# Half-line pads in the SBUF tiles of a one-core diffusion-block kernel

## The chip, the cores and the metric

The kernel runs on one NeuronCore of a Trainium2 chip. The metric is the time of one execution on the device in microseconds (us). Before the change three runs gave 1022.84, 1023.95 and 1025.29 us, median 1023.95 us.

## The reference, cut to what matters

One block of a diffusion backbone runs over 256 latent tokens and 256 context tokens of width 1024; only the latent stream is returned.

```python
x   = x   + 0.5 * g1x * swiglu(modulate(rmsnorm(x, n1), sh1x, sc1x), w13_1, w2_1)     # 512 tokens:
ctx = ctx + 0.5 * g1c * swiglu(modulate(rmsnorm(ctx, n1), sh1c, sc1c), w13_1, w2_1)   # x and ctx
q, k, v, g, f, ga, gf = project(modulate(rmsnorm(x, n2), ...), w_in)                   # ctx: k, v only count
o = bidir_retention(rope(q), rope(k), v, ...)          # 4 heads, decays, states of the context
r = (silu(g) * groupnorm(o)) @ p_ret
fo = fft2(f).real @ p_four
x = x + g2x * ((sigmoid(ga) * r + sigmoid(gf) * fo) @ w_out)
x = x + 0.5 * g3x * swiglu(modulate(rmsnorm(x, n3), ...), w13_2, w2_2)
return rmsnorm(x, n_final)
```

All of it is in float32. The feed-forward width is 2816, `w_in` has 9216 columns.

## The kernel before

Activations stand transposed: 128 channels on the partitions, tokens along the free dimension, eight such tiles for 1024 channels. Every large product is done by `mm3` (lines 86 to 90): weight and activation are each split into a high part of the type float32r and the rest (`load_w`, lines 70 to 80, and `split`, lines 82 to 84), and three matmuls are added up in PSUM: low weight by high activation (L88), high by low (L89), high by high (L90). In each the 128 by 128 piece of weights is the stationary operand, loaded by an LDWEIGHTS of its own, and the activation streams past it. The activation has 512 columns where both streams run (the first feed-forward), 256 where one does, and 258 in the second feed-forward, whose tiles `hx` carry two more columns for a shift (line 856). In `fourier_in` the roles are exchanged: tokens are stationary and 512 columns of weights stream. In scores, `u_unit` and the Fourier units both operands are activations.

The stages, by the name of the bank that they write: `acc`, `pa`, `pb` (up, first feed-forward) and `y` (down), 512 columns; the last two column tiles of the second half of `y` are done as four units of 256 columns (`late`, lines 405 to 416). Then, with 256 columns: for each of four heads `kc`, `kx`, `q` (projections), `s` (scores), `u` (keys by scores, line 561), `o` (line 655), with the 512-column `f` in the last head; `g` (gates) among `sq` and `mx` (Fourier by tokens and by channels); `gg` and `ro` (merge); `yo` (output projection, line 865). Then `fa` and `fb` with 258 columns (22 units, line 890), and `z` with 256 (8 units of 66 matmuls, line 923). The order of instructions on each engine is made when the program is built, by a scheduler with a model of the chip; some matmuls of the next unit are drawn into the one before.

Weights come in pieces of 512 KB through one queue (SyncE) into `wr`, ScalarE makes the high part `wh`, VectorE (for some GpSimd) the low part `wl`; each has four buffers of 4096 bytes a partition.

**Where the tiles stand.** SBUF is given out in pools, from the left end (`per`, `wp`, `tp`, `hp`, `gp`, then `ttp` and `g2` in the place of `hp` and `gp`) and from the right (`mp`, `dp`, `mc`, `ap`, later `fp` and `mxp`), a pool's tiles one behind the other, each rounded up to 32 bytes. The place of a tile within a line of 128 bytes follows by addition. In this program all buffers of `wp` (`wr`, `wh`, `wl`) start 32 bytes into such a line; so do `h1`, `gh` and `gl`, `mg` (in the places of `tt`) and the first `hx`; all of their sizes but that of `hx` are whole lines, and so the places stay. `hx` tiles of 258 columns take 1032 bytes, rounded up to 1056, so that the sixteen stand at 32, 64, 96, 0, 32, ... ; behind them `g2h` and `g2l` are again at 32. `h2x` and `h2c`, all tiles of `ap` (`kt`, `qt`, `ut`, `pt`, `ht`), of `fp` (`dft`, `fu`, `cu`) and of `mxp` (`mx`, `gt`) stand at 96. Pieces of 128 columns of weights (512 bytes) and of 256 columns of activations (1024 bytes) are whole lines too, so a slice has its tile's place.

Of the kernel before, what the change touches and what calls it, by code (L numbers as in the profile page):

```python
# [8 lines left out]
F32R = mybir.dt.float32r  # L9
BF16 = mybir.dt.bfloat16  # L10
AF = mybir.ActivationFunctionType
ALU = mybir.AluOpType

P = 128
T = 256
D = 1024
KT = D // P
# [9 lines left out]
OUT = (P, KT, T)  # L27
UB = 4
HOOK = 0
TC_KW = dict(schedule_with_timeline_sim=True)  # L30


# [5 lines left out]
def block_kernel(ctx: ExitStack, tc: tile.TileContext, i: dict, out: bass.AP):  # L38
    nc = tc.nc
    V, S, G, PE = nc.vector, nc.scalar, nc.gpsimd, nc.tensor  # L40
# [9 lines left out]
    def fpool(stack, name, side):  # L50
        return stack.enter_context(tc.tile_pool(name=name, bufs=1, reuse_waits="tile", side=side))
# [4 lines left out]
    ada_stack = ExitStack()  # L56
    adp = fpool(ada_stack, "adp", "left")

    def bank(name):
        return psum.tile([P, 512], F32, name=name, tag="ps")  # L60

    def f32(ap):
        return ap.bitcast(F32)

    uid = [0]

    def wtile(t, name):
        return wp.tile([P, 1024], F32 if t == "wr" else F32R, name=name, tag=t, bufs=4)

    def load_w(src, n, lo_engine=None):  # L70

        uid[0] += 1
        raw, hi, lo = [wtile(t, f"{t}{uid[0]}") for t in ("wr", "wh", "wl")]
        dst = raw[:, :n]
        if len(src.shape) == 3:
            dst = dst.rearrange("p (k c) -> p k c", k=src.shape[1])
        nc.sync.dma_start(dst, src)
        S.copy(hi[:, :n], raw[:, :n])  # L78
        (lo_engine or V).tensor_tensor(lo[:, :n], raw[:, :n], f32(hi[:, :n]), op=ALU.subtract)  # L79
        return hi, lo  # L80

    def split(dst_hi, dst_lo, src):
        S.copy(dst_hi, src)
        V.tensor_tensor(dst_lo, src, f32(dst_hi), op=ALU.subtract)

    def mm3(o, w, a, start, stop):

        PE.matmul(o, w[1], a[0], start=start, stop=False)  # L88
        PE.matmul(o, w[0], a[1], start=False, stop=False)  # L89
        PE.matmul(o, w[0], a[0], start=False, stop=stop)  # L90

    def sl(pair, *idx):
        return pair[0][idx], pair[1][idx]
# [31 lines left out]
    for q in range(4):  # L125
        t = per.tile([P, 2, 512], F32, name=f"xs{q}")
# [33 lines left out]
    ct = stp.tile([P, 2, 4, 32], F32, name="ct")  # L160
    V.memset(ct, 0.0)
    ps = bank("ct")
    for c in range(4):
        PE.transpose(ps[:, c * P : (c + 1) * P], cr[:, c * P : (c + 1) * P], unit_raw)
# [156 lines left out]
    for k in range(KT):  # L321
# [3 lines left out]
        n = 2 * M1 * P  # L325
        hi, lo = wtile("wh", f"wh0_{k}"), wtile("wl", f"wl0_{k}")
# [16 lines left out]
    def some_ada(n):  # L343
        for _ in range(min(n, len(todo))):
            ada(*todo.pop(0))
# [12 lines left out]
                mm3(ps, sl(ws[k // 4], slice(None), slice(c, c + P)), h[k], k == 0, k == KT - 1)  # L358
        return gated_unit(pa, pb, f"1_{m}")

    def w2_chunks(src, kts):
        ws, k0 = [], 0
        for n in kts:
            w = load_w(src[:, k0 * P : (k0 + n) * P], n * P)
            ws += [sl(w, slice(None), slice(c * P, (c + 1) * P)) for c in range(n)]
            k0 += n
        return ws
# [3 lines left out]
    def add_sq(ap, cols, first, name):  # L371

        sq = tp.tile([P, 512], F32, name=f"sq{name}", tag="t2k", bufs=T2K)
        w = cols.stop - cols.start
        if first:
            S.activation(ssum[0][:, cols], ap, AF.Square)
            return
        S.activation(sq[:, :w], ap, AF.Square)  # L378
        G.tensor_tensor(ssum[0][:, cols], ssum[0][:, cols], sq[:, :w], op=ALU.add)  # L379

    def y_evac(ps, j, streams, st, col0):
        for n, s in enumerate(streams):
            c = slice(s * T, (s + 1) * T)
            V.scalar_tensor_tensor(
                xs[j][:, c], ps[:, col0 + n * T : col0 + (n + 1) * T], gate_col(st, s, j),
                xs[j][:, c], op0=ALU.mult, op1=ALU.add,
            )

    def ffn1_down(hf, gs, n_ada=0):
        late = []  # L390
        if hf:
            ssum[0] = per.tile([P, 512], F32, name="ssum2", tag="ssum")
        for j in range(KT):
            some_ada(n_ada)
            ws = w2_chunks(i["w2a"][hf, j], (6, 5))
            if hf and j >= KT - 2:
                late.append((j, ws))
                continue
            ps = bank(f"y{hf}_{j}")
            for k in range(HALF):  # L400
                mm3(ps, ws[k], gs[k], k == 0, k == HALF - 1)
            y_evac(ps, j, (0, 1), 0, 0)
            if hf:
                add_sq(xs[j], slice(0, 512), j == 0, f"2_{j}")
        for s in (0, 1):
            for j, ws in late:
                ps = bank(f"y{hf}_{j}_{s}")
                c = slice(s * T, (s + 1) * T)
                for k in range(HALF):
                    mm3(ps[:, :T], ws[k], sl(gs[k], slice(None), c), k == 0, k == HALF - 1)  # L410
                    if (s, j, k) == (1, KT - 2, 3):
                        norms.append(stage2_norm(0))
                y_evac(ps, j, (s,), 0, 0)
                sq = tp.tile([P, T], F32, name=f"sq2_{j}_{s}", tag="t1k", bufs=2)
                S.activation(sq, xs[j][:, c], AF.Square)
                late_sq[s].append(sq)
# [3 lines left out]
    def stage2_norm(s):  # L420
        ps = bank(f"st2_{s}")
        PE.matmul(ps[:, :T], ones, ssum[0][:, s * T : (s + 1) * T], start=True, stop=False)
        for n, sq in enumerate(late_sq[s]):
            PE.matmul(ps[:, :T], ones, sq, start=False, stop=(n == 1))
        return rstd_of(ps[:, :T], T, f"2_{s}")
# [54 lines left out]
    def decays(hd):  # L480
# [16 lines left out]
    raw = tp.tile([P, P], F32, name="unit_2", tag="t1k", bufs=2)  # L497
# [10 lines left out]
    ]  # L508

    ttp = fpool(ctx, "ttp", "left")  # L510
    tt = [ttp.tile([P, 512], F32, name=f"tt{n}", tag=f"tt{n}") for n in range(2 * HEADS)]
    ap = fpool(heads, "ap", "right")
    rope = ap.tile([P, 2, T], F32, name="rope")
    nc.sync.dma_start(rope, i["rope"])
    cos2, sin2 = [rope[:, n, :].unsqueeze(1).to_broadcast([P, 2, T]) for n in range(2)]
    keys, query, sums, probs = [
        [[ap.tile([P, 512], F32R, name=f"{nm}{n}_{x}") for x in range(2)] for n in range(cnt)]
        for nm, cnt in (("kt", 2), ("qt", 1), ("ut", UB), ("pt", 2))
    ]

    ht = [[ap.tile([P, D], F32R, name=f"ht{t}_{x}") for x in range(2)] for t in range(4)]

    def two(a):
        return a.rearrange("p (a t) -> p a t", a=2)
# [9 lines left out]
    def transposed(s, k, banks):  # L534

        for t in range(2):
            for x in range(2):
                if k % 4 == 0:
                    banks[t, x] = bank(f"ht{s}_{t}_{x}_{k}")
                c = slice((k % 4) * P, (k % 4 + 1) * P)  # L540
                PE.transpose(
                    banks[t, x][:, c].bitcast(F32R), (hc2, hx2)[s][k][x][:, t * P : (t + 1) * P], unit
                )
        if k % 4 == 3:
            c = slice((k // 4) * 512, (k // 4 + 1) * 512)
            for t in range(2):
                S.copy(ht[2 * s + t][0][:, c], banks[t, 0])
                S.copy(ht[2 * s + t][1][:, c], banks[t, 1])

    def first_unit(s, w, a, pss, hook=None):  # L550

        banks = {}
        for k in range(KT):
# [3 lines left out]
            transposed(s, k, banks)  # L557
            if hook and k == HOOK:
                hook()
# [122 lines left out]
    fs, fu, cu, mx = {}, [], [], []  # L682

    def fourier_open():
        heads.close()
        fs["fp"] = fp = fpool(mix, "fp", "right")
        dft = [fp.tile([P, 768], F32R, name=f"dft{n}") for n in range(2)]
        for n in range(2):
            raw = tp.tile([P, 512], F32, name=f"dftr{n}", tag="t2k", bufs=T2K)
            c = slice(n * 384, (n + 1) * 384)  # L690
            nc.sync.dma_start(raw[:, :384], i["dft"][:, c])
            split(dft[0][:, c], dft[1][:, c], raw[:, :384])
        fs["dft"] = dft
        for n in range(2):
            fu.append([[fp.tile([P, 512], F32R, name=f"fu{n}_{e}_{x}") for x in range(2)] for e in range(2)])
        fs["cu"] = [
            [fp.tile([P, 512], F32R, name=f"cu{n}_{x}") for x in range(2)] for n in range(4)
        ]
        mxp = fpool(mix, "mxp", "right")
        for tiles, nm, cnt in ((mx, "mx", 4), (gt, "gt", KT)):  # L700
            for n in range(cnt):
                tiles.append([mxp.tile([P, 512], F32R, name=f"{nm}{n}_{x}") for x in range(2)])
# [118 lines left out]
    for j in range(KT):  # L821
        ws = [load_w(i["wgate"][j, c], 1024) for c in range(2)]
# [6 lines left out]
        wr = [load_w(i["pret"][j, c], 1024) for c in range(2)]  # L829
# [26 lines left out]
    W = T + 2  # L856
    g2 = fpool(ctx, "g2", "left")
    hx = [
        (g2.tile([P, W], F32R, name=f"hxh{k}"), g2.tile([P, W], F32R, name=f"hxl{k}"))
        for k in range(KT)  # L860
    ]
    ssum[0] = per.tile([P, 512], F32, name="ssum3", tag="ssum")
# [60 lines left out]
    for j in range(KT):  # L923
        ws = w2_chunks(i["w2b"][j], (8, 8, 6))
# [124 lines left out]
```

## Time and profile before

| | |
|---|---|
| median of 3 runs | 1023.95 us |
| profiled execution | 1024.28 us, of which its span 1022.5 us |
| TensorE matmuls (PE) | 983.2 us busy, 96% of the span, 6792 instructions |
| weight loads (PEld) | 907.0 us, 89% |
| VectorE (DVE), ScalarE (ACT), GpSimd (POOL) | 65%, 46%, 6% |
| granted TensorE clock | 0.993 on average |
| HBM read | 164.70 MB, 162 GB/s over the span |

A row of a profile names the line of the kernel, the engine, the operation, output and inputs by tile names without numbers, the partitions and elements, the count, busy time and the mean duration of one in ns. The duration of a matmul contains its way through the array and overlaps that of its neighbours; how fast they follow each other is read from how many fall into a stretch.

### The profile page before, as it was taken

The numbers are of one execution on the slowest core, as the hardware profiler recorded it, in microseconds if no ns is written. First come the engines' busy times: TensorE is split into PE (matmuls) and PEld (weight loads), VectorE is DVE, ScalarE is ACT, GpSimd is POOL, SyncE is SP. The second block draws the span as 40 slices with busy tenths as digits, with TensorE's granted clock in tenths as the row PEclk, the third lists the DMA queues.
The fourth block names the chain that finished last, engine by engine and source line by source line (L and its number), as shares of the span: only waits on it lengthen the run. The fifth ranks groups of instructions, "written<-read, shape, count | busy, mean of one in ns | idle before, by whom it ended". The sixth has DMA issues, their size and how long they took to land.

```text
span 1022.5 us, 16777 instructions
## 1 busy us (share of the span) xinstructions
PE 983.2 (96%) x6792; PEld 907.0 (89%) x6792; DVE 661.5 (65%) x1083; ACT 469.1 (46%) x725; POOL 62.3 (6%) x39
## 2 busy tenths in 40 slices
PE   4899999999999999999999998999999989999996
PEld 3668888888888889899999997999999989999995
DVE  7938999998332434875575637955555767667543
ACT  5444232223422423755476457754445545554541
POOL 0000000000000013100000007000000210000011
PEclk9999999999999999899999999999999999999999
DMA  8727766996232233224132625455666555656651
GB/s 345 246 76 250 226 208 197 317 409 235 83 111 70 86 89 110 83 85 125 60 124 63 201 65 163 125 172 187 197 186 187 165 164 171 186 181 174 185 179 42
DMA packets 49238, 166.84 MB, mean 163 GB/s; under 512 B 5380, under 2 KB 7044, under 8 KB 49160
## 3 DMA queue, kind: packets, MB, share of 16 engines
q1 hardware_dynamic: 49160, 165.77, 50.8%
q8 instruction: 53, 0.87, 0.3%
q14 instruction: 25, 0.20, 0.1%
HBM read 164.70 MB, written 1.05 MB: 162 GB/s over the span
## 4 chain that ended last, share of the span: by engine, by line
PE 89%; DVE 4%; ACT 3%; issue 1%; DMA 1%; POOL 0%; SPq 0%; DVEq 0%; ACTq 0%; POOLq 0%
PE y L88 4%; PE y L89 4%; PE y L90 4%; PE pa L88 3%; PE pa L89 3%; PE pb L89 3%; PE pa L90 3%; PE pb L90 3%; PE pb L88 3%; PE ro L89 2%; PE ro L90 2%; PE ro L88 2%; PE fa L89 2%; PE z L90 2%; PE z L88 2%; PE z L89 2%
## 5 line engine op out<-in xcount | busy, mean ns | idle before, releaser
L79 DVE TENSOR_TENSOR wl<-wr,wh 128x1024 fp32r<-128x1024 f32 (+1 forms) x214 | 249.0, 1164 | 203.0 <-ACT wh L78 202.1
L78 ACT CAST wh<-wr 128x1024 fp32r<-128x1024 f32 (+1 forms) x226 | 226.9, 1005 | 281.6 <-PE y L90 79.2
L181 DVE CUSTOM_DVE_ANT_0 junk<-ada,cb,sm 128x1024 bf16<-128x1024 f32 x96 | 122.8, 1280 | 5.3 <-DMA ada<-in_ada 4.5
L89 PE MATMUL y<-gl,wh 128*128 128x512 f32 (+1 forms) x198 | 72.5, 366 | 0.0
L88 PE MATMUL y<-gh,wl 128*128 128x512 f32 (+1 forms) x198 | 72.4, 366 | 0.0
L90 PE MATMUL y<-gh,wh 128*128 128x512 f32 (+1 forms) x198 | 72.3, 365 | 0.0
L379 POOL TENSOR_TENSOR ssum<-ssum,sq 128x256 f32<-128x256 f32 (+1 forms) x18 | 24.5, 1362 | 736.0 <-ACT sq L378 722.8
L88 PE MATMUL pa<-h1h,wl 128*128 128x512 f32 x152 | 59.2, 390 | 0.0
L89 PE MATMUL pa<-h1l,wh 128*128 128x512 f32 x152 | 59.1, 389 | 0.0
L90 PE MATMUL pa<-h1h,wh 128*128 128x512 f32 x152 | 59.1, 389 | 0.0
L88 PE MATMUL pb<-h1h,wl 128*128 128x512 f32 x152 | 59.1, 389 | 0.0
L89 PE MATMUL pb<-h1l,wh 128*128 128x512 f32 x152 | 59.1, 389 | 0.0
L90 PE MATMUL pb<-h1h,wh 128*128 128x512 f32 x152 | 59.1, 389 | 0.0
L89 PE MATMUL fa<-hxl,wh 128*128 128x258 f32 x176 | 50.9, 289 | 0.0
L88 PE MATMUL fa<-hxh,wl 128*128 128x258 f32 x176 | 50.8, 289 | 0.0
L90 PE MATMUL fa<-hxh,wh 128*128 128x258 f32 x176 | 50.6, 288 | 0.0
L89 PE MATMUL fb<-hxl,wh 128*128 128x258 f32 x176 | 50.1, 284 | 0.0
L89 PE MATMUL z<-g2l,wh 128*128 128x256 f32 x176 | 50.0, 284 | 0.0
L88 PE MATMUL fb<-hxh,wl 128*128 128x258 f32 x176 | 50.0, 284 | 0.0
L90 PE MATMUL fb<-hxh,wh 128*128 128x258 f32 x176 | 49.9, 283 | 0.0
L88 PE MATMUL z<-g2h,wl 128*128 128x256 f32 x176 | 49.8, 283 | 0.0
L90 PE MATMUL z<-g2h,wh 128*128 128x256 f32 x176 | 49.8, 283 | 0.0
(309 smaller groups left out, 2896.5 us busy)
## 6 DMA issues: line engine op xcount, KB each, us to landing
ada<-in_ada SPq DMA_DIRECT2D x72, 512.0 KB, 5.2
wr<-in_w13b SPq DMA_DIRECT2D x44, 512.0 KB, 4.4
wr<-in_w13a SPq DMA_DIRECT2D x38, 512.0 KB, 4.2
wrv<-in_wv SPq DMA_DIRECT2D x16, 512.0 KB, 4.5
wr<-in_wg SPq DMA_DIRECT2D x16, 512.0 KB, 3.8
wr<-in_wgate SPq DMA_DIRECT2D x16, 512.0 KB, 4.4
wr<-in_pret SPq DMA_DIRECT2D x16, 512.0 KB, 3.7
wr<-in_w2b SPq DMA_DIRECT2D x16, 512.0 KB, 3.6
```

Source lines behind the costliest of these rows:

```text
L78: S.copy(hi[:, :n], raw[:, :n])
L79: (lo_engine or V).tensor_tensor(lo[:, :n], raw[:, :n], f32(hi[:, :n]), op=ALU.subtract)
L88: PE.matmul(o, w[1], a[0], start=start, stop=False)
L89: PE.matmul(o, w[0], a[1], start=False, stop=False)
L90: PE.matmul(o, w[0], a[0], start=False, stop=stop)
L181: V.tensor_tensor_reduce(junk, raw, cb[:, s, :], 1.0, sm[:, BIAS + n : BIAS + n + 1], ALU.mult, ALU.add, mod[:, s, n : n + 1],)
L379: G.tensor_tensor(ssum[0][:, cols], ssum[0][:, cols], sq[:, :w], op=ALU.add)
```

## The change

`padded` allocates a tile with 16 more float32 columns (64 bytes) and hands out the part without them, so that what stands behind it moves by 64 bytes. It is used for the last `kt`, `qt`, `pt` and `ht` of `ap`, and in `fp` for `dft1` and the last `cu`. At the head of `ttp` a tile `edge` of 48 columns (192 bytes, 64 more than a line) is added and 32 of its columns are set to zero once by VectorE. `hx` tiles get 288 columns of room (1152 bytes, nine lines) for the 258 used. In the four late units of `y` the weights are put 64 bytes into their buffers (`at`).

```diff
+LINE = 32
+    def padded(pool, n, name):
+        return pool.tile([P, n + LINE // 2], F32R, name=name)[:, :n]
-    def load_w(src, n, lo_engine=None):
+    def load_w(src, n, lo_engine=None, at=0):
-        raw, hi, lo = [wtile(t, f"{t}{uid[0]}") for t in ("wr", "wh", "wl")]
+        raw, hi, lo = [wtile(t, f"{t}{uid[0]}")[:, at : at + n] for t in ("wr", "wh", "wl")]
...
-            ws = w2_chunks(i["w2a"][hf, j], (6, 5))
-            if hf and j >= KT - 2:
+            in_two = hf and j >= KT - 2
+            ws = w2_chunks(i["w2a"][hf, j], (6, 5), LINE // 2 if in_two else 0)
+            if in_two:
...
     ttp = fpool(ctx, "ttp", "left")
+    V.memset(f32(padded(ttp, LINE, "edge")), 0.0)
...
-        [[ap.tile([P, 512], F32R, name=f"{nm}{n}_{x}") for x in range(2)] for n in range(cnt)]
+        [
+            [
+                (padded(ap, 512, f"{nm}{n}_{x}") if (n, x) == (cnt - 1, 1) and nm != "ut"
+                 else ap.tile([P, 512], F32R, name=f"{nm}{n}_{x}"))
+                for x in range(2)
+            ]
+            for n in range(cnt)
+        ]
         for nm, cnt in (("kt", 2), ("qt", 1), ("ut", UB), ("pt", 2))
...
+        [(padded(ap, D, f"ht{t}_{x}") if (t, x) == (3, 1) else ap.tile([P, D], F32R, name=f"ht{t}_{x}"))
+         for x in range(2)]
+        for t in range(4)
...
-        dft = [fp.tile([P, 768], F32R, name=f"dft{n}") for n in range(2)]
+        dft = [fp.tile([P, 768], F32R, name="dft0"), padded(fp, 768, "dft1")]
...
+            [(padded(fp, 512, f"cu{n}_{x}") if (n, x) == (3, 1) else fp.tile([P, 512], F32R, name=f"cu{n}_{x}"))
+             for x in range(2)]
+            for n in range(4)
...
-        (g2.tile([P, W], F32R, name=f"hxh{k}"), g2.tile([P, W], F32R, name=f"hxl{k}"))
+        tuple(g2.tile([P, LINE * -(-W // LINE)], F32R, name=f"{nm}{k}")[:, :W] for nm in ("hxh", "hxl"))
```

## Rows read from the trace of the kernel before

**Rows 1.** The page: busy us, share of the span, instructions; granted clock in 40 slices.
```profile
PE 983.2 (96%) x6792; PEld 907.0 (89%) x6792; DVE 661.5 (65%) x1083; ACT 469.1 (46%) x725; POOL 62.3 (6%) x39
PEclk9999999999999999899999999999999999999999
```
**Rows 2.** Matmuls by stretch (us): length, PE busy (count), granted clock, DMA share, GB/s.
```profile
605.00:620.80 15.80, 15.80 (x141) 1.00 0.69 206
680.00:780.00 100.00, 100.00 (x851) 1.00 0.62 189
850.00:940.00 90.00, 90.00 (x742) 1.00 0.61 180
960.00:1000.00 40.00, 40.00 (x335) 1.00 0.55 167
```
**Rows 3.** Matmuls grouped by line and shape, 605 to 620: o of the last head.
```profile
L89 PE MATMUL o<-ut,whv 128*128 128x256 f32 x32 | 8.8, 276 | 0.0
```
**Rows 4.** The same for 680 to 780: gg and ro.
```profile
L89 PE MATMUL gg<-h2xl,wh 128*128 128x256 f32 x115 | 32.3, 281 | 0.0
L89 PE MATMUL ro<-gt,wh 128*128 128x256 f32 x112 | 31.5, 281 | 0.0
```
**Rows 5.** The same for 850 to 940: fa.
```profile
L88 PE MATMUL fa<-hxh,wl 128*128 128x258 f32 x125 | 35.5, 284 | 0.0
```
**Rows 6.** The same for 960 to 1000: z.
```profile
L88 PE MATMUL z<-g2h,wl 128*128 128x256 f32 x111 | 31.4, 283 | 0.0
```
**Rows 7.** The same over the whole span: the groups that the change moves (L90 of each).
```profile
L90 PE MATMUL fa<-hxh,wh 128*128 128x258 f32 x176 | 50.6, 288 | 0.0
L90 PE MATMUL z<-g2h,wh 128*128 128x256 f32 x176 | 49.8, 283 | 0.0
L90 PE MATMUL u<-pt,ht 128*128 128x256 f32 x128 | 36.1, 283 | 0.0
L90 PE MATMUL yo<-mg,wh 128*128 128x256 f32 x64 | 18.1, 283 | 0.0
L90 PE MATMUL y<-gh,wh 128*128 128x256 f32 x44 | 12.4, 283 | 0.0
L90 PE MATMUL s<-qt,kt 128*128 128x256 f32 x32 | 9.0, 283 | 0.0
L90 PE MATMUL mx<-cu,dft 128*128 128x256 f32 x16 | 4.5, 282 | 0.0
```
**Rows 8.** The same for 437.9 to 443.2, before the first scores, then 443.6 to 445.3, behind two.
```profile
L89 PE MATMUL kx<-h2xl,wh 128*128 128x256 f32 x16 | 4.4, 276 | 0.0
...
L89 PE MATMUL kc<-h2cl,wh 128*128 128x256 f32 x5 | 1.4, 281 | 0.0
```
**Rows 9.** The same for 490.2 to 494.9, behind fp32 matmuls, then 507 to 522, behind u.
```profile
L89 PE MATMUL kc<-h2cl,wh 128*128 128x256 f32 x14 | 3.9, 276 | 0.0
...
L89 PE MATMUL q<-h2xl,wh 128*128 128x256 f32 x16 | 4.5, 281 | 0.0
```
**Rows 10.** The same for two stretches of 512 columns: 180 to 220 and 569.9 to 579.9.
```profile
L88 PE MATMUL y<-gh,wl 128*128 128x512 f32 x60 | 23.3, 389 | 0.0
L88 PE MATMUL f<-wh,h2xl 128*128 128x512 f32 x15 | 5.8, 397 | 0.0
```
**Rows 11.** Matmuls in order of time, 814.5 to 815: start, duration.
```profile
814.61 0.28 PE L88 MATMUL fa<-hxh,wl 128*128 128x258 f32 x1
814.73 0.28 PE L89 MATMUL fa<-hxl,wh 128*128 128x258 f32 x1
814.85 0.28 PE L90 MATMUL fa<-hxh,wh 128*128 128x258 f32 x1
814.97 0.29 PE L88 MATMUL fa<-hxh,wl 128*128 128x258 f32 x1
```
**Rows 12.** All engines by stretch: PE, PEld, DVE, ACT, POOL busy us (count).
```profile
640.00:650.00 10.00, 10.00 (x88) 10.00 (x87) 10.00 (x15) 7.75 (x11) 0.00 (x0) 1.00 0.25 84
810.00:820.00 10.00, 9.35 (x78) 9.14 (x77) 9.94 (x20) 6.59 (x12) 5.45 (x3) 1.00 0.55 168
860.00:880.00 20.00, 20.00 (x166) 20.00 (x166) 13.98 (x28) 10.49 (x14) 0.00 (x0) 1.00 0.59 173
```
**Rows 13.** TensorE's waits, 600 to 850: us in total, times, longest.
```profile
PE st L898 <- POOL ssum L379: 3.0, 1, 3.0
```
**Rows 14.** VectorE grouped by line, 800 to 820: its smallest operation there.
```profile
L878 DVE COPY xa<-sh 128x2 f32<-128x2 f32 x7 | 1.0, 158 | 0.0
```

More of the change, by code (lines that the diff above doesn't have):

```diff
@@ L68, in wtile @@
         return wp.tile([P, 1024], F32 if t == "wr" else F32R, name=name, tag=t, bufs=4)
-    def load_w(src, n, lo_engine=None):
+    def load_w(src, n, lo_engine=None, at=0):
         uid[0] += 1
-        raw, hi, lo = [wtile(t, f"{t}{uid[0]}") for t in ("wr", "wh", "wl")]
-        dst = raw[:, :n]
+        raw, hi, lo = [wtile(t, f"{t}{uid[0]}")[:, at : at + n] for t in ("wr", "wh", "wl")]
+        dst = raw
         if len(src.shape) == 3:
@@ L77, in load_w @@
         nc.sync.dma_start(dst, src)
-        S.copy(hi[:, :n], raw[:, :n])
-        (lo_engine or V).tensor_tensor(lo[:, :n], raw[:, :n], f32(hi[:, :n]), op=ALU.subtract)
+        S.copy(hi, raw)
+        (lo_engine or V).tensor_tensor(lo, raw, f32(hi), op=ALU.subtract)
         return hi, lo
@@ L359, in ffn1_up, with w2_chunks @@
         return gated_unit(pa, pb, f"1_{m}")
-    def w2_chunks(src, kts):
+    def w2_chunks(src, kts, at=0):
         ws, k0 = [], 0
         for n in kts:
-            w = load_w(src[:, k0 * P : (k0 + n) * P], n * P)
+            w = load_w(src[:, k0 * P : (k0 + n) * P], n * P, at=at)
             ws += [sl(w, slice(None), slice(c * P, (c + 1) * P)) for c in range(n)]
@@ L516, in block_kernel @@
     keys, query, sums, probs = [
-        [[ap.tile([P, 512], F32R, name=f"{nm}{n}_{x}") for x in range(2)] for n in range(cnt)]
+        [
[6 more added lines that the diff above has]
+        ]
         for nm, cnt in (("kt", 2), ("qt", 1), ("ut", UB), ("pt", 2))
     ]
-    ht = [[ap.tile([P, D], F32R, name=f"ht{t}_{x}") for x in range(2)] for t in range(4)]
+    ht = [
+        [(padded(ap, D, f"ht{t}_{x}") if (t, x) == (3, 1) else ap.tile([P, D], F32R, name=f"ht{t}_{x}"))
+         for x in range(2)]
+        for t in range(4)
+    ]
     def two(a):
@@ L696, in fourier_open @@
         fs["cu"] = [
-            [fp.tile([P, 512], F32R, name=f"cu{n}_{x}") for x in range(2)] for n in range(4)
+            [(padded(fp, 512, f"cu{n}_{x}") if (n, x) == (3, 1) else fp.tile([P, 512], F32R, name=f"cu{n}_{x}"))
+             for x in range(2)]
+            for n in range(4)
         ]
```

## The prediction

> **What bounds the kernel now.** I read the page's first two parts, then the matmuls grouped by stretch and shape, the counts of matmuls per stretch, and only then waits and the other engines. TensorE is busy for 96% of the span at the full granted clock [rows 1], and its longest wait behind the heads is 3.0 us [rows 13]. So the time is the sum of 6792 matmuls times the pace at which they follow each other, and the question is whether that pace can change.
>
> The paces differ between stretches that do the same work. A stretch's count holds about two matmuls that had begun before it; without them 960 to 1000 us has 333 in 40 us, 120.1 ns each; 680 to 780 has 849 in 100 us, 117.8 ns; 605 to 620.8 has 139 in 15.8 us, 113.7 ns [rows 2]. All three are 256 columns on 128 by 128 weights, with no wait and at clock 1.00. The mean durations beside them are 283, 281 and 276 ns [rows 3, 4, 6]: each is the pace plus 163 (276 gives 113). So the pace of any group is its mean duration less 163, and I use 120, 118 and 113.5.
>
> Now the places of the tiles in their 128-byte lines, from the list of pools above. z streams `g2` (32) past weights at 32: same place, 283. u streams `pt` (96) past `ht` (96), yo `mg` (32) past 32, s `qt` (96) past `kt` (96), y `gh` (32) past 32: same place, and each 283; mx, 96 past 96, 282 [rows 7]. gg, ro, o, q, kc, kx stream a tile at 96 past weights at 32: half a line apart, and these have 281 or 276 [rows 3, 4, 8, 9]. No group of 256 columns in the same place has a steady pace under 120, none half a line apart a steady one over 118. This is what the change acts on.
>
> Half a line apart has two paces, and which it takes depends on what went before. kx runs at 276; then two score matmuls (same place) come, and kc, half a line apart as before, runs at 281 [rows 8]. Behind the fp32 matmuls of a norm kc has 276 again, then u (same place) follows, and q and o behind it have 281 to the end of the head [rows 9]. Behind the 512-column f, o has 276 [rows 3]. From 680 to 780 nothing interrupts and the pace of 118 persists for 849 matmuls [rows 2, 4]. So a pause or 512 columns let the pair fall into the fast pace, matmuls in the same place push it into the middle one, and it does not come back by itself.
>
> The Trainium skill speaks against all this: its page "TensorE: Matmul & The Clock Gate", section "Step-by-step: what each phase is for", says that TensorE has two independent read ports and that loading the next weights does not take bandwidth from the running matmul. By that the place of an operand would be of no account and the time would stay 1024; the trace differs, with 283 against 281 and 276 for one shape [rows 3, 4, 6].
>
> **The change part by part.** Places after it, by addition: in `ap` three pads of 64 bytes alternate the groups and the fourth keeps the pool's length at whole lines, so `kt`, `ut`, `pt` stay at 96, `qt` and `ht` go to 32. `edge` puts `mg`, `hx` and `g2` at 96, and `hx` at nine lines each leaves all sixteen there. `fu` and `cu` go to 32, `dft`, `mx`, `gt` stay. The late y weights go to 96 beside `gh` at 32. So z, fa, fb, u, yo, s, sq, mx and late y are all half a line apart; the 512-column groups are untouched.
>
> Added work: one memset of 32 columns on VectorE. The smallest row is 158 ns [rows 14]; it is issued at the start of the heads, where 0 to 0.2 us can fall on the path; I take 0. No DMA, wait or bank is added, and the tiles that `edge`, `hx` and `g2` cover had their last readers long before. The pads cost memory alone.
>
> What is gained, matmul by matmul:
> - z, 3 x 176 = 528 [rows 7], with no same-place work ahead of it any more. From 120 to 113.5 that is 3.4 us; from 120 to 118, 1.1.
> - fa and fb: 6 x 176 = 1056 [rows 7]. With `hx` at four places the pace is 740 in 90 us, 121.6 ns [rows 2], and the duration 284 agrees within a ns [rows 5]. No row shows 258 columns steadily half a line apart. The nearest is the start of fa, where hx0 and the weights stand in the same place: starts 0.12 us apart [rows 11], as 256 columns do there. So I take the pace of 256 plus two columns at 2.4 GHz (0.8 ns): 114.3, or 118.8 in the middle pace. Some 40 come before the 3.0 us wait for `ssum` and only lengthen it. 1016 x 7.3 = 7.4 us, or 1016 x 2.8 = 2.8. Bounds: 113.5 below; above, the difference of the 512-column rows, in the rival below.
> - u: 3 x 128 [rows 7], 96 a head. In heads 1 to 3 a pause stands ahead (fp32 matmuls or f), so 288 x 6.5 = 1.9; in head 0 same pace as its surroundings, 96 x 2 = 0.2.
> - q and o of heads 1 and 2, which u no longer disturbs: 288 matmuls from 118 to 113.5 [rows 9], 1.3 us.
> - late y: 3 x 44 = 132 [rows 7] behind 512 columns, 0.9 us at most; what follows is the chain of norm and modulation on VectorE and ScalarE, which starts from a matmul half way through, so 0.5.
> - s, sq, mx: 96 + 48 + 48 = 192 from 120 to 118: 0.4, of which waits in the Fourier units keep some; 0.3.
> - yo: 192 matmuls, but VectorE is busy 9.94 of 10 us there [rows 12] and decides the end through `ssum` [rows 13]. Only the first evacuation comes earlier: 0.2 instead of 1.2.
>
> s and mx are the awkward ones: there the weights are at 96 and the stream at 32, so on the way in a stream at 96 runs while weights at 96 load, and on the way out 32 beside 32: two single steps in the same place, at each. I take it that these push the pair into the middle pace, as two matmuls did in rows 8, and that g3 to g7, gg and ro therefore stay at 118.
>
> Sum: 3.4 + 7.4 + 2.1 + 1.3 + 0.5 + 0.3 + 0.2 = 15.2 us. The profiled execution took 1024.28, its span 1022.5; less 15.2 it is 1009.1. It lies 0.33 above the median, so 1008.8. Nothing else comes late at that pace: in fa VectorE has 13.98 and ScalarE 10.49 of 20 us [rows 12], and DMA 0.61 [rows 2].
>
> **The rivals.**
> The fast pace holds through s and mx. Then kc1, q1, o0, kx2, kx3 (288), u0 (96), s, sq, mx (192) and g3 to g7, gg, ro (1200) gain 4.5 ns more each, 1776 x 4.5 = 8.0 us, less 0.8 in 640 to 660 where VectorE is full at 10.00 of 10 [rows 12] and would be waited for: 1001.6. For it: 849 matmuls without one change of pace [rows 2]; against it: rows 8.
>
> The last third locks at the middle pace: fa starts again behind the 3.0 us wait [rows 13], and no row shows 258 columns half a line apart settling behind one. Then fa and z give 3.9 instead of 10.8: 1015.7. The middle pace everywhere: z 1.1, fa 2.8, u 0.8, y and s 0.5, together 5.2: 1018.7.
>
> It does nothing: the three paces come from something else that goes with the stage, and the time stays 1024. Against it: five groups in the same place have one duration in five stages [rows 7]. The page of the Trainium skill named above would have this outcome.
>
> Slower: half a line apart hurts where the stream is longer than the load of weights. With 512 columns y (same place) has 389 and f (half a line apart, roles exchanged) 397 [rows 10]: 8 ns more, the other way round than with 256. If 258 columns behave as 512 do, fa and fb go from 121.6 to 120.8 + 8 = 128.8, 1056 x 7.2 = 7.6 us more, against 2.4 of the others at the middle pace: 1029.1. It decides as soon as the 258 lose more than the rest wins, some 2.3 ns each. Against it: rows 11, where 258 behave as 256.
>
> **How the numbers follow.** The sum 0.38; the fast pace throughout 0.22; the last third at the middle pace 0.17; the middle pace everywhere 0.10; nothing 0.05; slower by 258 columns 0.05; 0.03 for something in the heads that I do not see. The first four reach from 1001.6 to 1018.7 with 0.87; with a microsecond for the roundings of the paces the range is 1000.5 to 1019.5. 0.2% is 2 us, about what this kernel's runs can tell from no change. Faster by more: the first four and a little of the rest, 0.88; within: 0.06; slower: 0.06.
>
> **What would show it.** Mean durations of z, u, yo, s near 276 or 281 instead of 283; fa near 277 or 282 instead of 284; q and o of heads 1 and 2 at 276. gg and ro at 281 would show that s and mx push the pace, 276 that they do not. fa above 285 would be the slower case. The prediction is wrong where z keeps 283, or where the durations fall and the span does not, because waits take their place.

## The result, and the profile after

The changed kernel takes 1017.71 us (median of four runs, 1017.31 to 1019.31), the kernel before beside it 1023.39 (1022.61 to 1025.29): a ratio of 0.9945 with the 95% interval 0.9927 to 0.9963, some 5.7 us faster. The direction was right and the time lies within the range; the size of the gain was not right: 15.2 us were forecast. The profiled execution took 1019.31 us (span 1017.5, 5.0 less than the span of before). All medians and ratios here are of executions in the fast state; one of the seven of `pause_before_gg`, 2488.69 us, is left out of them.

The page, against [rows 1]: busy us, share and instructions, and the granted clock in 40 slices. 6.6 us of matmul time are gone.

```profile
PE 976.6 (96%) x6792; PEld 900.1 (88%) x6792; DVE 662.8 (65%) x1084; ACT 469.0 (46%) x725; POOL 62.5 (6%) x39
PEclk9999999999999999899999999999999989999999
```

Matmuls by stretch, as [rows 2]: length, PE busy (count), granted clock, DMA share, GB/s: gg and ro, then fa and fb, then z.

```profile
675.00:775.00 100.00, 100.00 (x864) 1.00 0.65 193
850.00:940.00 90.00, 90.00 (x752) 1.00 0.61 183
960.00:1000.00 40.00, 40.00 (x342) 1.00 0.49 147
```

By the prediction's count (two less) these are 116.0 ns for gg and ro (117.8 before), 120.0 for fa and fb (121.6) and 117.6 for z (120.1). The two that carried the sum, fa and z, each reached far less than forecast, and gg and ro, for which nothing was forecast, fell.

Matmuls of one tile over the whole span, against [rows 3 to 7]: count, then shortest, median and longest duration in ns, then the start of the first and of the last. With 256 columns a duration of 276 goes with 113.3 ns from start to start (the fast pace), 279 to 281 with 117.8 (the middle pace) and 283 with 120.0 (the slow pace).

```profile
L94 PE MATMUL o<-ut,whv x128: 279/280/281, 470.8 to 615.2; 128*128 128x256 f32 x128
L94 PE MATMUL gg<-h2xl,wh x128: 276/276/279, 677.6 to 780.2; 128*128 128x256 f32 x128
L94 PE MATMUL ro<-gt,wh x128: 280/280/280, 683.1 to 785.9; 128*128 128x256 f32 x128
L94 PE MATMUL yo<-mg,wh x64: 276/276/283, 789.0 to 810.6; 128*128 128x256 f32 x64
L93 PE MATMUL fa<-hxh,wl x176: 277/282/776, 810.8 to 941.2; 128*128 128x258 f32 x176
L94 PE MATMUL fa<-hxl,wh x176: 282/287/419, 810.9 to 941.3; 128*128 128x258 f32 x176
L95 PE MATMUL z<-g2h,wh x176: 276/281/281, 944.7 to 1006.8; 128*128 128x256 f32 x176
L95 PE MATMUL u<-pt,ht x128: 276/280/284, 456.0 to 592.9; 128*128 128x256 f32 x128
L95 PE MATMUL s<-qt,kt x32: 277/279/281, 447.8 to 570.1; 128*128 128x256 f32 x32
```

z, yo, u and s have left 283. yo is at 276 nearly throughout, z at 281 until the fp32 matmuls of the last norm, near its end. gg and ro, which had one duration in [rows 4], now differ, 276 and 280, though they alternate.

From the starts of the same rows in both traces comes where the 5.0 us of span were won (us; the first row lies before anything that the change touches):

| from, to | before | after | won | forecast |
|---|---|---|---|---|
| start, first y | 166.2 | 168.4 | -2.2 | 0 |
| first y, last y | 241.4 | 240.9 | 0.5 | 0.5 |
| last y, last o (heads) | 207.9 | 206.0 | 1.9 | 3.6 |
| last o, first gg (g, sq, mx) | 63.0 | 62.2 | 0.8 | 0.1 |
| first gg, last ro | 113.0 | 111.3 | 1.7 | 0 |
| last ro, first fa (yo) | 23.1 | 22.0 | 1.1 | 0.2 |
| first fa, first z | 133.6 | 133.6 | 0.0 | 7.4 |
| first z, last z | 63.6 | 62.4 | 1.2 | 3.4 |
| last z, end | 10.7 | 10.7 | 0.0 | 0 |

Two entries belong to this execution. The start was 2.2 us late (`hx_ten_lines`, below, has the first y at 166.0 with the same program up to there), which may be much of why the profiled run is the slowest of the four. And fa's gain against before's trace (967 matmuls by 1.6 ns, 1.5 us) was lost at its beginning. TensorE's wait there, against [rows 13]: us in total, times, longest.

```profile
PE st L918 <- POOL ssum L384: 3.7, 1, 3.7
```

Of yo's gain of 1.1 us 0.7 so came back as a longer wait: the chain to `ssum` decides, and not TensorE, as the prediction had it. Behind the wait the granted clock was at 0.50, the 1.2 GHz level, and longer than before. The matmuls by stretch there, after and then before:

```profile
816.80:818.80 2.00, 0.00 (x0) 0.81 0.88 320
818.80:820.80 2.00, 1.57 (x5) 0.50 0.97 338
820.80:822.80 2.00, 2.00 (x11) 0.50 0.14 57
822.80:824.80 2.00, 2.00 (x12) 0.50 0.00 0
```
```profile
822.60:824.60 2.00, 2.00 (x12) 0.67 0.62 242
824.60:826.60 2.00, 2.00 (x12) 0.50 0.00 0
```

In the first 15.4 us from fa's start before has 89 matmuls and after 75: 14 fewer, 1.7 us at 120 ns; the granted clock is 0.89 and 0.78 over them. Another execution with the places of after (`pause_before_z`, below) has 83 at 0.89, with the same wait of 3.7 us. So some 0.7 us are the longer wait, and the clock's part, some 1.0, is not a steady cost of the change.

Nor is 121.6 ns the steady pace of before's places. Three more executions with `hx` placed as in before, described below (`pause_before_gg`, then `ffn1_place_a` and `ffn1_place_b`), have, from 850 to 940, where before had 742:

```profile
850.00:940.00 90.00, 90.00 (x745) 1.00 0.57 180
850.00:940.00 90.00, 90.00 (x748) 1.00 0.56 183
850.00:940.00 90.00, 90.00 (x749) 1.00 0.57 183
```

That is 121.1, 120.6 and 120.5 ns. The places of after are worth 0.5 to 1.6 ns a matmul in fa, 0.5 to 1.7 us in all.

The rows that correspond to [rows 9, 10]: kx and q, which had the middle pace there in before (q 281 in [rows 9]), the late y, and the 512-column y and f of [rows 10]. Each stretch grouped by line, 485 to 491, 508 to 513.3, 406.5 to 409.2, 180 to 220 and 594 to 604:

```profile
L94 PE MATMUL kx<-h2xl,wh 128*128 128x256 f32 x16 | 4.4, 276 | 0.0
...
L94 PE MATMUL q<-h2xl,wh 128*128 128x256 f32 x16 | 4.4, 276 | 0.0
...
L95 PE MATMUL y<-gh,wh 128*128 128x256 f32 x9 | 2.5, 276 | 0.0
...
L93 PE MATMUL y<-gh,wl 128*128 128x512 f32 x59 | 23.0, 389 | 0.0
...
L94 PE MATMUL f<-wl,h2xh 128*128 128x512 f32 x15 | 5.9, 394 | 0.0
L95 PE MATMUL f<-wh,h2xh 128*128 128x512 f32 x15 | 5.8, 388 | 0.0
```

f won 4.4 ns a matmul by the steps between starts (its durations were 397 [rows 10]) although neither of its operands was moved. Late y is the group of which the weights alone were moved, and the stream was not. It left 283 all the same, so what counts is how the two operands stand to each other, not where the stream stands by itself.

### The profile page after: what moved, and what is told of

It is laid out like the page before. It is cut to its first block, busy times and chain, and to the rows that moved or that the text cites. A ratio compares the mean times of both kernels' runs of the same rounds, so it can differ in the third digit from the quotient of the medians.

```text
span 1017.5 us, 16778 instructions
## 1 busy us (share of the span) xinstructions
PE 976.6 (96%) x6792; PEld 900.1 (88%) x6792; DVE 662.8 (65%) x1084; ACT 469.0 (46%) x725; POOL 62.5 (6%) x39
## 4 chain that ended last, share of the span: by engine, by line
PE 90%; DVE 4%; ACT 2%; DMA 1%; issue 1%; POOL 0%; SPq 0%; DVEq 0%; ACTq 0%; POOLq 0%
PE y L93 4%; PE y L94 4%; PE y L95 4%; PE pa L93 3%; PE pa L94 3%; PE pb L94 3%; PE pb L93 3%; PE pa L95 3%; PE pb L95 3%; PE ro L94 2%; PE ro L93 2%; PE ro L95 2%; PE fa L94 2%; PE fa L95 2%; PE fb L94 2%; PE z L93 2%
```

## The experiments

**Place** here is the start of the stream less the start of the weights, modulo 256 bytes, by addition of the tiles' sizes. Where one operand lies in the pools of the left end and one in those of the right, the sizes alone do not tell 64 from 192; 192 is taken for gg and its like in before because `kc` falls to 276 behind fp32 matmuls [rows 9], as z does at 192 and not at 64 (`tail_at_64`). In before, z, u, yo, s, y and mx have place 0, and gg, ro, o, q, kc, kx and g place 192; the tiles of `hx` are spread over all eight multiples of 32. In after, z, yo, u, late y, gg, q, kc, kx and g have 192, but ro, o, s and mx have 64; and since nine lines are 1152 bytes, hx alternates: the high parts at 192, the low ones at 64. Theory A: the place counts modulo 256, 192 being able to run at 113 and 64 settling at 118. Theory B, the prediction's: only the place in a 128-byte line counts, and history chooses between 113 and 118. Each kernel ran beside the kernel before on its chip, and the ratio is to that.

**hx at one place.**
```diff
-        tuple(g2.tile([P, LINE * -(-W // LINE)], F32R, name=f"{nm}{k}")[:, :W] for nm in ("hxh", "hxl"))
+        tuple(g2.tile([P, 10 * LINE], F32R, name=f"{nm}{k}")[:, :W] for nm in ("hxh", "hxl"))
```


> The changed kernel with ten lines (1280 bytes) a tile for hx in place of nine, so that all sixteen stand at the same place in 256 bytes; the places in 128 bytes are those of the changed kernel. Theory A (the pace goes by the place of the stream behind the weights in 256 bytes: 0 gives 120 ns, 64 always 118, 192 either 118 or 113.5 by what went before): hx no longer alternates between 64 and 192, so fa and fb fall from 120.0 to 118.8 or 114.3 and z stays at 117.8 or falls to 113.5; 1016.5 us or 1009.6 us in place of 1017.7. Theory B (only the place in 128 bytes counts): nothing moves, 1017.7.

1016.59 us, ratio 0.9922 (0.9907 to 0.9937). The three matmuls of a product in fa and fb become alike (in after, 280, 285 and 283 ns in the same stretch), and z stays. Grouped by line, 850 to 930 and 960 to 990:
```profile
L93 PE MATMUL fa<-hxh,wl 128*128 128x258 f32 x110 | 31.2, 284 | 0.0
L94 PE MATMUL fa<-hxl,wh 128*128 128x258 f32 x109 | 30.9, 284 | 0.0
...
L95 PE MATMUL z<-g2h,wh 128*128 128x256 f32 x86 | 24.2, 281 | 0.0
```
With every hx at 192, 258 columns take 120.8 ns, neither 114.3 nor 118.8: the mixed places were not what kept fa slow. This ratio's interval overlaps with that of after.

**The tail at 64.** On top of that, an edge of 64 bytes puts yo, fa, fb and z at place 64.
```diff
-    V.memset(f32(padded(ttp, LINE, "edge")), 0.0)
+    V.memset(f32(ttp.tile([P, 16], F32R, name="edge")), 0.0)
```


> As the kernel with ten lines for hx, but edge takes 64 bytes in place of 192: mg, hx and g2 stand 64 bytes behind the weights in 256 bytes, not 192; in 128 bytes they are half a line apart as before. Theory A: yo goes from 113.5 to 118, fa and fb are at 118.8, z at 117.8 to its last matmul, also behind the fp32 matmul of the last norm, where the changed kernel has 113.7: about 1016.5 us. Theory B: the same as with 192, whatever that is.

1017.6 us, ratio 0.9927 (0.9911 to 0.9944). The end of z, behind the fp32 matmuls of the norm, grouped by line, here (1004.5 to 1009) and then in after (1003.6 to 1007.5):
```profile
L95 PE MATMUL z<-g2h,wh 128*128 128x256 f32 x10 | 2.8, 279 | 0.0
```
```profile
L95 PE MATMUL z<-g2h,wh 128*128 128x256 f32 x10 | 2.8, 276 | 0.0
```
At 192 z falls to 276 behind those fp32 matmuls (a pause, from here on), at 64 it does not; both are half a 128-byte line apart. fa and fb took 122.2 ns here, more than the 120.8 at 192. This speaks for A.

**Everything at 192.** Other pads bring ro, o, s and mx to 192 too, with the hx of ten lines.
```diff
+    def padded(pool, n, name, pad=LINE // 2):
...
-                (padded(ap, 512, f"{nm}{n}_{x}") if (n, x) == (cnt - 1, 1) and nm != "ut"
+                (padded(ap, 512, f"{nm}{n}_{x}", 48 if nm == "kt" else 16) if (n, x) == (cnt - 1, 1) and nm != "ut"
...
+        [(padded(ap, D, f"ht{t}_{x}", 48) if (t, x) == (3, 1) else ap.tile([P, D], F32R, name=f"ht{t}_{x}"))
...
+            fu.append([[padded(fp, 512, f"fu{n}_{e}_{x}", 32 if (n, e, x) == (1, 1, 1) else 0) for x in range(2)] for e in range(2)])
```


> Ten lines for hx, and other pads in ap and fp (192 bytes behind kt and ht, 64 behind qt and pt, 64 behind dft, 128 behind fu, 64 behind cu), so that all matmuls of 256 and 258 columns stream 192 bytes behind their weights in 256; in the changed kernel s, o, mx and ro are at 64. Theory A: s, o, mx and ro (1104 matmuls) can go from 117.8 to 113.5, up to 4.7 us less than with ten lines alone, 1005 us where fa and z are fast too. Theory B: o and ro stay at 117.8, the same time as with ten lines alone.

1014.44 us, ratio 0.9902 (0.9887 to 0.9917). Grouped by line, 675 to 775 and 945 to 1000, then the whole span of o:
```profile
L94 PE MATMUL gg<-h2xl,wh 128*128 128x256 f32 x119 | 32.8, 276 | 0.0
L94 PE MATMUL ro<-gt,wh 128*128 128x256 f32 x112 | 30.9, 276 | 0.0
...
L95 PE MATMUL z<-g2h,wh 128*128 128x256 f32 x161 | 44.4, 276 | 0.0
```
```profile
L94 PE MATMUL o<-ut,whv x128: 276/281/281, 469.3 to 614.7; 128*128 128x256 f32 x128
```
ro at 192 has 276 where ro at 64 had 280, between units of gg at 276 in both. But o stays at 281 in most heads, at 192 as well: the place allows the fast pace and does not give it. z is fast here behind the same fa that it was not in hx_ten_lines.

**A pause in the kernel before.** Nothing is moved; one fp32 matmul, whose result is not used, goes ahead of gg.
```diff
+        if j == 0:
+            PE.matmul(bank("pause")[:, :T], ones, xs[0][:, :T], start=True, stop=True)
```


> The kernel before with one fp32 matmul of 256 columns (two passes, its output unused) ahead of gg0. There gg and ro stand at 192 and run at 117.8 for 960 matmuls. If the pace is a state that what went before sets and that lasts, the break lets it fall to 113.5 until yo, which is in the same place: 960 x 4.3 = 4.1 us less, 0.5 more for the break, 1019.8 us. If the stage itself sets the pace, gg and ro stay at 281 ns in duration and the time is 1023.9.

1020.49 us (six runs), ratio 0.996 (0.9947 to 0.9973). Grouped by line, 680 to 780, against [rows 4]:
```profile
L89 PE MATMUL gg<-h2xl,wh 128*128 128x256 f32 x127 | 35.1, 276 | 0.0
L89 PE MATMUL ro<-gt,wh 128*128 128x256 f32 x112 | 30.9, 276 | 0.0
```
One matmul ahead changes the pace of the 960 behind it, which are at 117.8 in all four traces with these places and no pause (before, `tail_only`, `ffn1_place_a` and `ffn1_place_b`). That is the state of the prediction, by itself, at places that no pad has touched.

**fa and fb with 256 columns.** All at 192; the two columns for the shift are not computed, other data stand in for them.
```diff
-                mm3(p_[:, :W], sl(ws[k // 4], slice(None), slice(c, c + P)), hx[k], k == 0, k == KT - 1)
+                mm3(p_[:, :T], sl(ws[k // 4], slice(None), slice(c, c + P)), sl(hx[k], slice(None), slice(0, T)), k == 0, k == KT - 1)
```


> As all_192, but fa and fb stream 256 of the 258 columns; the two columns of the shift are left out and another column stands in for the shift. Places and the order of work are as in all_192, where fa and fb run at 120.8 ns at 192 throughout. Theory A (258 columns take another pace than 256 in the same place): 113.3 or 117.8 ns, 7.9 or 3.2 us less than the 1014.4 of all_192, 1006.5 or 1011.2. Theory B (something else of that stage holds it: its tiles, VectorE, the transfers): it stays at 120.8, only the clock of two columns less, 0.9 us.

1008.07 us, ratio 0.9851 (0.9825 to 0.9876).

**264 and 272 columns.** On the version with pauses below; the further columns are zeros, and the small tile that fills them grows with them.
```diff
...
-    W = T + 2
+    W = T + 8          # and T + 16
...
```


> Built on the version with every matmul of 256 or 258 columns at 192 bytes of 256 and a pause ahead of u in heads 0 to 2 (1011.2 us; fa and fb, 1056 matmuls of 258 columns, at 120.8 ns each). Here those 1056 matmuls have 264 columns (1056 bytes of each line of hx): the further columns are zeros and their results are not used; every other place stays. Theory A (what costs is a row of the stream that does not end on a whole block: 258 columns are 1032 bytes, 264 are 1056, 33 whole blocks of 32 bytes): fa and fb fall to 113.4 + 6 columns at most, 113 to 116 ns, and the time to 1004 to 1006 us. Theory B (each column past 256 costs in its own right, or the first one past it does): fa and fb at 120.8 to 123.3 ns (six columns more at 2.4 GHz are 2.5 ns), 1011 to 1014 us.

> The same with 272 columns (1088 bytes, 17 blocks of 64). Theory A with blocks of 64 bytes: fa and fb at 113.4 to 119 ns (16 columns more at 2.4 GHz are 6.7 ns past 256's 113.4), 1004 to 1010 us, and the run with 264 columns stays near 121. Theory B: fa and fb 5.8 ns (14 columns) over 258's 120.8, some 126.6 ns, 1017 us. If the pace grows with the columns from 256 on by what the extra columns take in both runs, and 258 alone stands above that line, the odd width is the cost; if 264 and 272 stand on a line through 258's, it is the step past 256.

1011.5 us, ratio 0.9869 (0.9842 to 0.9896), and 1015.78, ratio 0.9903 (0.9876 to 0.9931). The matmuls from 840 to 930 with 256, 258 (the version with pauses), 264 and 272 columns:
```profile
840.00:930.00 90.00, 90.00 (x796) 1.00 0.62 195
```
```profile
840.00:930.00 90.00, 90.00 (x747) 1.00 0.59 180
```
```profile
840.00:930.00 90.00, 90.00 (x752) 1.00 0.59 181
```
```profile
840.00:930.00 90.00, 90.00 (x732) 1.00 0.59 179
```
Less two each that is 113.4, 120.8, 120.0 and 123.3 ns. Two columns cost 7.4, the next six less than nothing (-0.8), the next eight 3.3, which is eight columns at 2.4 GHz. A row of a whole number of 32-byte blocks does not bring the 113 back, so theory A of these two runs falls; B, that the columns past 256 cost in their own right, is nearer, yet 264 came out 0.8 ns under its lower end and 272 3.3 ns under its 126.6. The 4.6 us that the last run takes more than the version with pauses (1011.23) are not all fa's: its z ran at 281, while that with 264 columns and that with pauses alone ran at 276.

**The tail alone.** Edge and nine-line hx in the kernel before, no pads in the heads and Fourier units, late y as before.
```diff
+    V.memset(f32(ttp.tile([P, 48], F32R, name="edge")[:, :32]), 0.0)
...
+        tuple(g2.tile([P, 288], F32R, name=f"{nm}{k}")[:, :W] for nm in ("hxh", "hxl"))
```


> The kernel before with edge and the nine lines of hx alone; ap, fp and late y as before. By the traces so far fa and fb come to 120.0 ns (1.7 us), z to 117.8 (1.2 us, or 3.5 if it falls to 113.3), yo to 113.5 without use, since VectorE decides there: 1021 us, about half of what the whole change gives; gg and ro stay at 192 and at 117.8 behind same-place work. If the heads' pads are not worth anything, the whole 5.6 us must be here: 1018.

1021.76 us (ten runs), ratio 0.9975 (0.996 to 0.9989): about half of the change's gain. Grouped by line, 680 to 780 and 960 to 1000:
```profile
L89 PE MATMUL gg<-h2xl,wh 128*128 128x256 f32 x115 | 32.3, 281 | 0.0
...
L90 PE MATMUL z<-g2h,wh 128*128 128x256 f32 x114 | 32.0, 281 | 0.0
```
z has after's pace and gg still before's: what took gg to 276 in after came from the pads of the heads and Fourier units (or the late y).

**The first feed-forward, moved.** In the kernel before, 64 bytes ahead of h1 and 64 more ahead of gh (a), or 192 and 128 (b), one profile each.
```diff
+    V.memset(hp.tile([P, 16], F32, name="hpad"), 0.0)    # b: 48
+    V.memset(gp.tile([P, 16], F32, name="gpad"), 0.0)    # b: 32
```


> The kernel before with 64 bytes ahead of h1 and 64 more ahead of gh: acc, pa, pb stream 64 bytes behind their weights in 256, the 512-column y 128; before, all stand at 0 and run at 226.7 ns. Theory A (the place counts with 512 columns too, the other way round, as f with 229 to 233 at 64 suggests): pa and pb 229 to 233, y at 128 as at 0, 226.7; 2 to 6 us more. Theory B (f is slower because the roles are exchanged): pa, pb and y stay at 226.7.

> The kernel before with 192 bytes ahead of h1 and 128 more ahead of gh: acc, pa, pb at 192, the 512-column y at 64. Theory A: y 229 to 233 as f; pa and pb at 192 either as at 64 or nearer the 215 that two columns less per line would allow, not known. Theory B: all stay at 226.7.

1032.03 and 1034.48 us, one execution each, so only the paces are read. Grouped by line, a from 200 to 240 (y at 128) and 300 to 340 (pb at 64); then b from 200 to 240 (y at 64), 300 to 340 (pa at 192) and 402 to 409 (late y at 64):
```profile
L90 PE MATMUL y<-gh,wh 128*128 128x512 f32 x46 | 18.1, 394 | 0.0
...
L90 PE MATMUL pb<-h1h,wh 128*128 128x512 f32 x30 | 11.8, 392 | 0.0
```
```profile
L89 PE MATMUL y<-gl,wh 128*128 128x512 f32 x48 | 18.8, 392 | 0.0
...
L89 PE MATMUL pa<-h1l,wh 128*128 128x512 f32 x32 | 12.7, 396 | 0.0
...
L89 PE MATMUL y<-gl,wh 128*128 128x256 f32 x21 | 5.8, 276 | 0.0
```
By the steps between starts, 512 columns take 226.7 ns at place 0 (before and after), 228.9 at 64, 232.4 at 128 and 233.4 at 192: 0 is the best place for them, and 128 is not the same as 0, so a period of 128 bytes falls for 512 columns. The last row is against theory A in its strict form: 256 columns at 64, steady, at 276, until a pause, behind which they have 281. The late y at 128, in a, has the 120.0 of place 0.

**A pause ahead of z, in after.**
```diff
+        if j == 0:
+            PE.matmul(bank("pause")[:, :T], ones, xs[0][:, :T], start=True, stop=True)
```


> The changed kernel with one fp32 matmul of 256 columns (output unused) ahead of z0. In the changed kernel z stands at 192 and runs at 117.8 behind fa, and at 113.7 only behind the fp32 matmul of the last norm in z7. If the pace is a state that lasts, z runs at 113.3 from its first matmul: 500 x 4.5 = 2.2 us less, 0.5 more for the break, 1016.0 in place of 1017.7. If z is at 117.8 for its own tiles' sake: 1018.2 and 281 ns.

1017.05 us, ratio 0.9923 (0.9905 to 0.9941). Grouped by line, 950 to 1000, and o of the last head, 600 to 615:
```profile
L95 PE MATMUL z<-g2h,wh 128*128 128x256 f32 x143 | 40.2, 281 | 0.0
...
L94 PE MATMUL o<-ut,whv 128*128 128x256 f32 x32 | 8.8, 276 | 0.0
```
The pause did not take: z keeps 281 until the norm's own fp32 matmuls. So a pause does not always free the pair, and the last o, at place 64 in both, is at 276 here and 280 in after, with no edit ahead of it and the same matmuls in the same order. The choice can fall either way between two executions. The first kx shows it too: 281 in after, but in `hx_ten_lines`, which is the same up to there, from 438 to 443, and here as well:
```profile
L95 PE MATMUL kx<-h2xh,wh 128*128 128x256 f32 x16 | 4.4, 276 | 0.0
```

**All at 192, with pauses in the heads.** An fp32 matmul, result unused, ahead of u in heads 0 to 2.
```diff
+        if hd < HEADS - 1:
+            PE.matmul(bank(f"pause{hd}")[:, :T], ones, xs[0][:, :T], start=True, stop=True)
```


> all_192 with an fp32 matmul of 256 columns ahead of u in heads 0 to 2, where u, q and o (240 matmuls a head) run at 117.8 at 192. If a break lets the pair fall to 113.3 and nothing behind it pushes, 3 x (240 x 4.5 - 0.5 us) = 1.7 us less than the 1014.4 of all_192, 1012.7. If the breaks do not take (kc2 and kc3 in all_192 run at 117.8 behind the fp32 matmuls of a norm), 1.4 us more, 1015.8.

1011.23 us (1010.94 to 1011.51), ratio 0.9862 (0.9846 to 0.9879): faster than both kernels, some 14 us less than before. The tiles over the whole span:
```profile
L94 PE MATMUL u<-pt,ht x128: 276/276/283, 453.6 to 590.1; 128*128 128x256 f32 x128
L94 PE MATMUL o<-ut,whv x128: 276/276/280, 468.6 to 612.2; 128*128 128x256 f32 x128
L94 PE MATMUL s<-qt,kt x32: 281/281/283, 445.2 to 566.9; 128*128 128x256 f32 x32
L95 PE MATMUL z<-g2h,wh x176: 276/276/281, 938.5 to 998.5; 128*128 128x256 f32 x176
```
Here the pauses took: the medians of u and o are 276, those of all_192 281 (o above, u alike). 256 columns at 192 run at 113.3 in most stages; some, as s, kx of heads 2 and 3 and u of the last head, stay at 117.8.

## Why the prediction was right in direction and wrong in size

- **What bounds, and that the place acts.** Right: the same 6792 matmuls in the same order became faster, every group that left place 0 left 283, and the rival that it does nothing is out. The rule of the Trainium skill quoted in the prediction ("TensorE: Matmul & The Clock Gate", "Step-by-step: what each phase is for"), by which loading the next weights takes nothing from the running matmul, left no room for that. This case's traces differ from it: moving operands alone took 256 columns from 120 to 117.8 or 113.3; no run looks at the two ports by themselves.
- **fa and fb, 7.4 us forecast.** This step failed, and it is the largest part of the error. "So I take the pace of 256 plus two columns at 2.4 GHz (0.8 ns): 114.3" rested on starts 0.12 us apart [rows 11], where 258 columns look as 256 do; rows in hundredths of a microsecond cannot tell 120 from 120.8, and only the high part `hxh0` stands there at place 0, while `hxl0` of the second row is 32 bytes on. Half a line apart 258 columns measured 120.0 in after and 120.8 with all at 192, and 256 columns in the same loop 113.4 (`fa_of_256`). The place is worth at most 1.6 ns there, not 7.3: what 256 columns gain by it, 258 do not. The rival of 258 columns had the right suspicion, that width matters, but made a loss of what was a missing gain.
- **z, 3.4 us forecast.** 1.2 measured: it locked at the middle pace behind fa. The step "with no same-place work ahead of it any more" took absence of such work for a reason to be fast. hx_ten_lines and all_192 have the same fa ahead and z at 281 and 276, and a pause did not free it in pause_before_z. Of the rivals the middle pace everywhere (1018.7) came nearest in time, with 1.1 for z, but not for its reasons: fa gave less than its 2.8 and gg more than its nothing.
- **gg, ro and g3 to g7, nothing forecast.** "I take it that these push the pair into the middle pace" failed: with s and mx at 64 the gates and gg fell to 276. gg won 384 x 4.4 = 1.7 us, in place of the 0 of the sum. ro stayed at 118, but not because s and mx pushed it, since gg between its units is at 276: the pads had put it at place 64, and with it at 192 (`all_192`) it has 276 too. That the time lies within the range is in part luck: without the 1.7 us of gg and the 0.8 of the gates, for which the sum had 0.1, it would have come out near 1020.1, above the range's 1019.5.
- **Heads, 3.6 us forecast, 1.9 measured.** u came out in the middle pace in heads 1 and 2 (2.2 of 6.5 ns), o in heads 1 and 2 not at all; o of the last head and q and kx at the beginning lost their fast pace (192 x 4.5 = 0.9 us). That loss is not a steady one: with the same places q and kx are fast in `hx_ten_lines` and `pause_before_z`, and the last o in `pause_before_z`. The line of 128 bytes hid that o moved from 192 to 64; that this kept it from 276 is not shown, since at 192 in `all_192` the o of heads 0 to 2 are at 281 as well.
- **yo.** Right: 1.1 us earlier, 0.7 of it taken back by the wait for `ssum` (1.0 of 1.2 forecast).

The law behind all terms was thus too coarse: the sum treated 64 and 192 as one place, and took a chance for a rule where either pace was possible. Both places have both paces, but not equally often. At 64, two stretches alone were at 113.3, late y in `ffn1_place_b` and the last o in `pause_before_z`; behind a pause 64 stayed at 117.8 (`tail_at_64`), where z at 192 fell to 113.3. With the places at 192 and the heads freed, some 14 of the forecast's 15.2 us are there, from other terms: gg, ro, u, q, o and z in place of fa.

**Still open.** What chooses between 113.3 and 117.8: neighbours at place 0, pauses, 512 columns and the place all move the odds, and none decides alone. Why two columns past 256 cost 7.4 ns and six more nothing. And what in the chip makes the pace depend on the place of one operand behind the other: no run here looks for the cause.

## What to carry to other kernels

When one shape has several paces in one trace, list the places of both operands beside each pace, with a modulus larger than the one you believe in, before pricing a pad. Price a shape that no row shows (258 columns) by a run of it alone, since two columns more undid here what the place gains. And where a pace is a state, a change of places gives a chance of the faster one, so count such terms at half and test with a pause in the old kernel first.

## What was not expected of the hardware

- Matmuls of 256 columns and 128 by 128 weights have three paces at the same granted clock of 1.00: 120.0 ns at places 0 and 128 (128 in `ffn1_place_a` alone), 117.8 or 113.3 at 192, 117.8 and twice 113.3 at 64. At 192 the choice can last for hundreds of matmuls (960 in `pause_before_gg`).
- For 512 columns the order is the other way: 226.7 ns at 0, 228.9 at 64, 232.4 at 128, 233.4 at 192. The 512-column f, which stands at 64 with the roles exchanged and was not moved, ran at 233.4 in before and 229.0 in after.
- 258, 264 and 272 columns take 120.8, 120.0 and 123.3 ns where 256 take 113.4.
- Behind one wait of 3.7 us, in after, the granted clock was at the 1.2 GHz level for more than 6 us; behind a wait of the same length in `pause_before_z` (0.57 and 0.58 in the two stretches of 2 us from 818 on, 1.00 behind them), and behind one of 3.0 in before, for little more than 3.
